# The low parts of the GLA gates' weights, made on GpSimd instead of VectorE

## The chip, the core and the metric

The kernel runs on one core of a Trainium2 chip. The metric is the device time of one execution in microseconds (us). The profile names the engines PE (TensorE; PEld is its weight load), DVE (VectorE), ACT (ScalarE), POOL (GpSimd) and SP (SyncE, which here does little but issue DMAs). Each engine works through a queue of its own in the order in which the program holds it: an instruction that waits holds up all that stand behind it.

## The reference

The program is a two-layer network on 512 tokens of width 1024, all in float32. Layer 0 mixes the tokens with an RWKV-7 recurrence (8 heads) and with gated linear attention (GLA, 4 heads), layer 1 with differential attention; a SwiGLU block follows each. The part that matters here:

```python
proj = h @ w_in
p_rkv = proj[..., :3 * RW_WIDTH]
gq, gk, gv, gg = jnp.split(proj[..., 3 * RW_WIDTH:], ...)
...
o = gla_chunked(...)                                  # 4 heads, 128 wide each
o_b = o.reshape(Bsz, T, GLA_VW).astype(h.dtype) * jax.nn.silu(gg)
return jnp.concatenate([o_a, o_b], axis=-1) @ w_out
```

`gg` is the GLA gates: 512 columns, four tiles of 128. `o_a` is the output of the RWKV-7 recurrence.

## The kernel before, in words

**Matrix products.** A float32 product is made of three faster ones. Each operand is split into a high part (a copy in a shorter format) and a low part (the rest): `split` makes the high part with a cast on ScalarE (L96, tile `whi`) and the low part with a subtraction on VectorE (L97, tile `wlo`). `mm3` then issues three matmuls: high by high (L107), high weight by low activation (L108), low weight by high activation (L109). `form_a` walks over the 1024 rows of a weight tile; in the first mixer it takes them in two pieces of 512 columns (256 KB), so that each tile of 128 outputs costs two DMAs (L84), two casts, two subtractions and 24 matmuls. The loaded pieces (`wraw`) live in a ring of three buffers: the fourth load can't start before the first piece's cast and subtraction are done. `whi` and `wlo` have rings of four here.

**The first mixer.** Token shifts and projections of RWKV-7 run chunk by chunk over four groups of two heads (class `Chunk`: `decays`, `project`, `key`, `receptance`, `value`, `gram`). In `shifted` the projection comes out of PSUM on VectorE (L501) and is scaled on ScalarE (L504, tile `d`); `value` uses `d` on VectorE (L556, L559); `gram` makes small matmuls (L547 belongs to `receptance`, L571 to `gram`), masks them on VectorE (L577) and moves them on ScalarE (L579 to L608).

**The two solves.** The recurrence needs the inverses of unit lower triangular blocks. `solve` computes them by 31 steps of a product (L633) and a sum (L635). The first solve (chunks 0 and 1, tiles `xl0`, `al0`, `tmp0`) runs on GpSimd, the second (chunks 2 and 3, tiles `xl2`, `al2`, `tmp2`) on VectorE. The second begins with a transpose (L624), which needs the last L608 of `gram` of chunk 3, and ends with a transpose (L638) and copies into place (L644, six of them on ScalarE).

**The gates.** `gla_gates` makes the four tiles of `gg`: a `form_a` each, a product with the row norms (L454), Silu (L455), a product with the GLA output on GpSimd (L458), and a DMA back to memory (L459). Its code stands between the last `gram` and the second solve. The output stage `rwkv_out` (L661, L663, L668, L670, ...) takes over the PSUM banks and the SBUF space of the gates, so it starts when they are done. Its copies into `st.fv` are L677 and L678, its state chain is L709, L712 (tile `H`, ScalarE), L714 (tile `S`, VectorE), and then L718 and L719 in turn.

**Order.** The code is recorded in program order; a scheduler with a cost model of its own then sets the order of each engine's queue, and adds the semaphore waits. So moving one kind of instruction to another engine can change the order of others.

Of the kernel before, what the change touches and what calls it, by code (L numbers as in the profile page):

```python
# [9 lines left out]
F32 = mybir.dt.float32  # L10
# [50 lines left out]
def dbank(g):  # L61
    return bank(g, "pd")
# [25 lines left out]
def split(g, raw, into=None):  # L88

    nc, n = g.nc, raw.shape[-1]  # L90
    if into:
        hi, lo = into
    else:
        hi = g.wp.tile([P, g.wn], F32R, name="whi", bufs=3 if g.wn > 512 else 4)[:, :n]
        lo = g.wp.tile([P, g.wn], F32R, name="wlo", bufs=3 if g.wn > 512 else 4)[:, :n]
    nc.scalar.copy(hi, raw)  # L96
    nc.vector.tensor_sub(lo, raw, hi.bitcast(F32))  # L97
    return hi, lo


# [347 lines left out]
def gla_gates(g, pool, ob):  # L448
    nc = g.nc
    for h in range(4):  # L450
        pg = dbank(g)
        form_a(g, pg, g.ap["win"][16 + h], g.xhi, g.xlo)
        gg = pool.tile([P, T], F32, name="gg", bufs=2)
        nc.vector.tensor_mul(gg, pg, g.rstd)  # L454
        nc.scalar.activation(gg, gg, AF.Silu)  # L455
        o = pool.tile([P, T], F32, name="o", bufs=2)
        nc.sync.dma_start(o, ob[h])
        nc.gpsimd.tensor_mul(o, o, gg)  # L458
        nc.sync.dma_start(ob[h], o)  # L459
# [722 lines left out]
def build(tc, ap, cols, dbg=None, parts=("mix0", "ffn0", "attn", "ffn1", "final")):  # L1182
    with ExitStack() as ctx:
        g = setup(ctx, tc, ap, dbg)
        g.cols, g.ahead = cols, 0
        if "mix0" in parts:
            mixer0(g)
        else:
            for c in range(KD):
                g.nc.sync.dma_start(g.xT[:, c], ap["xT"][:, c])  # L1190
        acts_pool(g, ctx, "xs")
        g.tbp = ctx.enter_context(tc.tile_pool(name="tb", bufs=1))
        g.tb = g.tbp.tile([P, NH_A, T], F32, name="tb")
        g.sqs = ctx.enter_context(tc.tile_pool(name="sqs", bufs=1))
        psum_pool(g, ctx, "ps", pd=3, sc=2, pt=2, po=1)
        weights_pool(g, ctx, 1024)
        if "ffn0" in parts:
            ffn(g, 0, bias_tables)
        if "attn" in parts:
            g.ahead = 120  # L1200
            attention(g)
            g.ahead = 0
        if "ffn1" in parts:
            ffn(g, 1, last=down_norm)
# [107 lines left out]
```

## Time and profile before

| | |
|---|---|
| time, median of 3 runs | 1336.83 us (1335.76 to 1337.07) |
| the profiled execution | 1336.43 us, its span 1334.6 us |
| PE busy | 1302.7 us, 98% |
| DVE busy | 701.3 us, 53% |
| ACT busy | 563.9 us, 42% |
| POOL busy | 216.3 us, 16% |
| L97 (all of them) on DVE | 252.4 us, 240 instructions |
| granted clock of PE, mean over the span | 0.992 |

Busy times overlap, since the engines run side by side. A share of the whole span says little about one stage: the stage of this change lies between 200 and 300 us, and is read there. Times of rows are counted from the start of the span. 1.83 us of the profiled execution lie around the span.

### The profile page before, as it was taken

To read this page: it belongs to the slowest core of one execution; us is meant where nothing else is said; L and a number is where in the kernel's file an instruction comes from. 1 tells how busy PE (TensorE), PEld (TensorE's weight loads), DVE (VectorE), ACT (ScalarE), POOL (GpSimd) and SP (SyncE) were. 2 spreads that over 40 slices of the span, in tenths; PEclk is the share of its full clock that TensorE was granted. 3 is DMA by queue.
4 is the path that set the end of the run, shared out by engine and by line. 5 is a ranking of instruction groups with operands and counts; after the bars stand their busy time and mean duration, and the time that the engine had idled before them with its cause. 6 is when DMAs were issued, how large, how long until landed. Compare 5 with 4: busy or idle time off the path is not lost.

```text
span 1334.6 us, 17753 instructions
## 1 busy us (share of the span) xinstructions
PE 1302.7 (98%) x6856; PEld 1065.9 (80%) x6856; DVE 701.3 (53%) x1197; ACT 563.9 (42%) x957; POOL 216.3 (16%) x205
## 2 busy tenths in 40 slices
PE   8999989899999999999999999999999999999998
PEld 6788767687878888888888887887888888888886
DVE  7465778954554433334434258888643434433342
ACT  5555866353443222223334347777432322322232
POOL 3011084211511110011112001110201110011110
PEclk9999989899999999999999999999999999999999
DMA  6222222423645323433234332211333323553331
GB/s 196 66 64 87 72 72 87 156 72 108 233 140 163 95 77 97 115 104 99 75 88 125 96 95 64 52 46 46 110 102 102 93 75 97 148 127 98 101 100 63
DMA packets 52719, 133.72 MB, mean 100 GB/s; under 512 B 6067, under 2 KB 8499, under 8 KB 52636
## 3 DMA queue, kind: packets, MB, share of 16 engines
q1 hardware_dynamic: 51772, 131.43, 32.8%
q8 instruction: 54, 0.88, 0.3%
q10 hardware_dynamic: 864, 1.17, 0.2%
q14 instruction: 29, 0.24, 0.1%
HBM read 121.74 MB, written 11.36 MB: 100 GB/s over the span
## 4 chain that ended last, share of the span: by engine, by line
PE 90%; DVE 7%; ACT 2%; issue 1%; DMA 0%; DVEq 0%; ACTq 0%
PE pd L109 24%; PE pd L108 24%; PE pd L107 24%; PE po L1054 2%; DVE wlo L97 1%; DVE tmp L633 1%; DVE xl L635 1%; PE sc L1029 1%; PE sc L1030 1%; PE o L109 1%; PE o L108 1%; PE o L107 1%; PE pt L1050 0%; PE o L675 0%; PE po L108 0%
## 5 line engine op out<-in xcount | busy, mean ns | idle before, releaser
L96 ACT CAST whi<-wraw 128x1024 fp32r<-128x1024 f32 (+2 forms) x240 | 210.4, 879 | 521.1 <-PE pd L108 302.0
L109 PE MATMUL pd<-xhi,wlo 128*128 128x512 f32 x1032 | 406.6, 394 | 0.0
L107 PE MATMUL pd<-xhi,whi 128*128 128x512 f32 x1032 | 405.6, 393 | 0.9 <-ACT xhi L188 0.9
L108 PE MATMUL pd<-xlo,whi 128*128 128x512 f32 x1032 | 405.8, 393 | 0.0
L97 DVE TENSOR_TENSOR wlo<-wraw,whi 128x1024 fp32r<-128x1024 f32 (+2 forms) x240 | 252.4, 1054 | 137.1 <-ACT whi L96 136.2
L107 PEld LDWEIGHTS pd<-xhi,whi 128*128 128x128 f32 x1032 | 193.8, 188 | 42.1 <-ACT xhi L188 1.3
L108 PEld LDWEIGHTS pd<-xlo,whi 128*128 128x128 f32 x1032 | 193.8, 188 | 41.1 <-issue 0.2
L109 PEld LDWEIGHTS pd<-xhi,wlo 128*128 128x128 f32 x1032 | 193.9, 188 | 40.4
L231 POOL TENSOR_TENSOR hlo<-h,hhi 128x512 fp32r<-128x512 f32 x44 | 67.3, 1529 | 546.3 <-ACT hhi L230 546.3
L227 DVE TENSOR_TENSOR ut<-pd,rstd 128x512 f32<-128x512 f32 x44 | 30.4, 692 | 146.3 <-PE pd L109 146.3
L107 PE MATMUL pd<-hhi,whi 128*128 128x512 f32 x264 | 102.7, 389 | 0.0
L108 PE MATMUL pd<-hlo,whi 128*128 128x512 f32 x264 | 102.7, 389 | 0.0
L109 PE MATMUL pd<-hhi,wlo 128*128 128x512 f32 x264 | 102.7, 389 | 0.0
L224 DVE TENSOR_TENSOR gt<-pd,rstd 128x512 f32<-128x512 f32 x44 | 30.4, 692 | 123.5 <-PE pd L109 121.4
L108 PEld LDWEIGHTS pd<-hlo,whi 128*128 128x128 f32 x264 | 49.6, 188 | 10.3
L107 PEld LDWEIGHTS pd<-hhi,whi 128*128 128x128 f32 x264 | 49.5, 188 | 10.3
L109 PEld LDWEIGHTS pd<-hhi,wlo 128*128 128x128 f32 x264 | 49.5, 188 | 10.3
L1034 ACT ACTIVATE s<-s,mn 128x384 f32<-128x384 f32 (+3 forms) x64 | 35.7, 559 | 21.4 <-DVE mn L1031 20.8
L230 ACT CAST hhi<-h 128x512 fp32r<-128x512 f32 x44 | 27.4, 622 | 35.5 <-DVE h L229 35.5
L240 DVE TENSOR_TENSOR xT<-pd,xT 128x512 f32<-128x512 f32 x24 | 16.6, 692 | 46.2 <-PE pd L109 46.2
L1010 POOL TENSOR_TENSOR qst<-q,qst 64x512 fp32r<-64x512 f32 x8 | 13.2, 1646 | 167.9 <-DVE qst L1008 167.9
L157 POOL TENSOR_TENSOR ssum<-nsq,ssum 128x512 f32<-128x512 f32 x21 | 31.5, 1498 | 49.9 <-ACT nsq L153 49.4
(384 smaller groups left out, 1837.4 us busy)
## 6 DMA issues: line engine op xcount, KB each, us to landing
wraw<-in_gate SPq DMA_DIRECT2D x44, 512.0 KB, 3.7
wraw<-in_up SPq DMA_DIRECT2D x44, 512.0 KB, 3.6
wraw<-in_win SPq DMA_DIRECT2D x40, 256.0 KB, 2.7
wraw<-in_down SPq DMA_DIRECT2D x24, 384.0 KB, 3.1
wraw<-in_wqk SPq DMA_DIRECT2D x16, 512.0 KB, 3.6
wraw<-in_down SPq DMA_DIRECT2D x24, 320.0 KB, 2.8
wraw<-in_downt SPq DMA_DIRECT2D x10, 512.0 KB, 3.7
xT<-in_xT SPq DMA_DIRECT2D x16, 256.0 KB, 3.9
```

The costliest lines, as they stand in the source:

```text
L96: nc.scalar.copy(hi, raw)
L97: nc.vector.tensor_sub(lo, raw, hi.bitcast(F32))
L107: nc.tensor.matmul(out, lhsT=lhi, rhs=rhi, start=start, stop=False)
L108: nc.tensor.matmul(out, lhsT=lhi, rhs=rlo, start=False, stop=False)
L109: nc.tensor.matmul(out, lhsT=llo, rhs=rhi, start=False, stop=stop)
L157: (nc.vector if c in fast else nc.gpsimd).tensor_add(ss, sq, first if c == 1 else ss)
L224: nc.vector.tensor_mul(gt, pg, rstd)
L227: nc.vector.tensor_mul(ut, pu, rstd)
L230: nc.scalar.copy(hhi[:, n], h)
L231: nc.gpsimd.tensor_sub(hlo[:, n], h, hhi[:, n].bitcast(F32))
L1034: nc.scalar.activation(s[:, m, :L], s[:, m, :L], AF.Exp, bias=mn[:, m:m + 1], scale=-1.0, accum_out=sm[:, m:m + 1])
L1054: nc.tensor.matmul(po[:, qb * P:qb * P + P], lhsT=att[:, b * P:b * P + P], rhs=v[:, b, h * P:h * P + P], start=b == 0, stop=b == qb)
```

## The change

```diff
@@ split
     nc.scalar.copy(hi, raw)
-    nc.vector.tensor_sub(lo, raw, hi.bitcast(F32))
+    g.low.tensor_sub(lo, raw, hi.bitcast(F32))
     return hi, lo
@@ gla_gates
     for h in range(4):
         pg = dbank(g)
+        g.low = nc.gpsimd
         form_a(g, pg, g.ap["win"][16 + h], g.xhi, g.xlo)
+        g.low = nc.vector
         gg = pool.tile([P, T], F32, name="gg", bufs=2)
@@ build
-        g.cols, g.ahead = cols, 0
+        g.cols, g.ahead, g.low = cols, 0, g.nc.vector
```

Eight subtractions of 128x512 (two for each of four tiles) change from VectorE to GpSimd. All others stay. Lines behind L451 of the kernel before stand two or three lines lower in the changed one (L458 is L460 there, L627 is L629, L633 is L635, L635 is L637, L644 is L646, L678 is L680, L712 is L714).

**First place: GpSimd's queue, from the end of the first solve to the last product of a gate.** `tmp0` and `xl0` belong to the first solve, `ga` is cleared for the inverses, `o` is a gate's GLA output. Before:

```order
L633 TENSOR_TENSOR tmp0_1560<-al0_1554,xl0_1551 128x31
L635 TENSOR_TENSOR xl0_1551<-xl0_1551,tmp0_1560 128x31
L627 MEMSET ga_1002 128x512 x4
L458 TENSOR_TENSOR o_2174<-o_2174,gg_2171 128x512
L458 TENSOR_TENSOR o_2218<-o_2218,gg_2215 128x512
L458 TENSOR_TENSOR o_2262<-o_2262,gg_2259 128x512
```

With the change:

```order
L637 TENSOR_TENSOR xl0_1551<-xl0_1551,tmp0_1560 128x31
L629 MEMSET ga_1002 128x512 x2
L97 TENSOR_TENSOR wlo_2138<-wraw_2135,whi_2137 128x512
L97 TENSOR_TENSOR wlo_2156<-wraw_2153,whi_2155 128x512
L97 TENSOR_TENSOR wlo_2182<-wraw_2179,whi_2181 128x512
L97 TENSOR_TENSOR wlo_2200<-wraw_2197,whi_2199 128x512
L629 MEMSET ga_1002 128x512
L97 TENSOR_TENSOR wlo_2226<-wraw_2223,whi_2225 128x512
L629 MEMSET ga_1002 128x512
L97 TENSOR_TENSOR wlo_2244<-wraw_2241,whi_2243 128x512
L460 TENSOR_TENSOR o_2174<-o_2174,gg_2171 128x512
L97 TENSOR_TENSOR wlo_2270<-wraw_2267,whi_2269 128x512
```

The eighth L97 (`wlo_2288`) follows the last row shown. All eight stand behind the whole first solve and two of the four memsets.

**Second place: ScalarE's queue at `value` of chunk 3.** `whi_2199` is the high part of the fourth gate piece, whose load (`wraw_2197`) takes the buffer of the first piece; `d_2044` is what `value` waits for. Before:

```order
L96 CAST whi_2181<-wraw_2179 128x512
L528 ACTIVATE a_1798<-a_1798,oka_282,vec_64 128x512
L96 CAST whi_2199<-wraw_2197 128x512
L504 ACTIVATE d_2044<-p_2041,omr_280 128x512
L96 CAST whi_2225<-wraw_2223 128x512
L579 COPY n21_1004<-ga_1002 32x2x128
L608 COPY dg_1013<-ga_1002 32x2x128 x2
```

With the change:

```order
L96 CAST whi_2181<-wraw_2179 128x512
L530 ACTIVATE a_1798<-a_1798,oka_282,vec_64 128x512
L96 CAST whi_2199<-wraw_2197 128x512
L506 ACTIVATE d_2044<-p_2041,omr_280 128x512
L581 COPY n21_1004<-ga_1002 32x2x128
L610 COPY dg_1013<-ga_1002 32x2x128 x2
```

The cast of `whi_2199` stands ahead of `d_2044` in both; the cast of `whi_2225` went behind the L608s.

**Third place: ScalarE's queue at the end of the second solve.** `dg` holds the solve's result; `o0` is a PSUM bank of the output stage of chunk 0, `xT` its result, `H_2542` its part of the state chain. Before:

```order
L676 COPY r_1000<-o0_2471 128x4x64
L678 COPY xT_63<-o0_2471 64x256
L712 COPY H_2542<-o0_2525 128x512
L908 CAST ghi_2410<-o_3189 128x512
L644 COPY ga_1002<-dg_1013 32x2x4x32 x6
```

With the change:

```order
L678 COPY r_1000<-o0_2471 128x4x64
L646 COPY ga_1002<-dg_1013 32x2x4x32 x6
L680 COPY xT_63<-o0_2471 64x256
L910 CAST ghi_2410<-o_3189 128x512
L714 COPY H_2542<-o0_2525 128x512
```

The six copies that wait for the second solve stood behind chunk 0's last copies, and now stand ahead of two of them. In VectorE's queue the gates' last L454 stood behind 34 instructions of the second solve's steps, and now stands behind 41.

## Rows read from the trace of the kernel before

**Rows 1.** Busy time by stretch: start:end, length, engines' busy us, PEclk, DMA share, GB/s.

```profile
212.00:216.00 4.00, 3.91 (x17) 2.82 (x15) 4.00 (x8) 1.95 (x3) 3.61 (x8) 1.00 0.40 131
...
244.00:248.00 4.00, 0.52 (x3) 0.08 (x1) 3.90 (x7) 1.35 (x3) 1.31 (x1) 1.00 0.44 140
...
268.00:272.00 4.00, 2.89 (x16) 2.78 (x17) 3.04 (x7) 3.54 (x8) 0.81 (x1) 0.76 0.00 0
272.00:276.00 4.00, 4.00 (x74) 3.80 (x75) 2.08 (x6) 2.15 (x6) 0.00 (x0) 0.81 0.46 135
```

**Rows 2.** The chain in order of time, 196 to 300 us: start, us, what.

```profile
229.34 0.63 ACT whi L96
229.99 0.69 DVE wlo L97
...
233.84 1.39 DVE wlo L97
...
237.25 0.60 DVE wlo L97
```

**Rows 3.** Timeline of POOL: start, us, engine, line, operation, tiles [idle before, releaser].

```profile
214.92 0.25 POOL L635 TENSOR_TENSOR xl<-xl,tmp 128x31 f32<-128x31 f32 x1
215.11 0.99 POOL L627 MEMSET ga<- 128x512 f32 x2
...
238.00 1.30 POOL L458 TENSOR_TENSOR o<-o,gg 128x512 f32<-128x512 f32 x1 [3.31 <-ACT gg L455]
```

**Rows 4.** The page's costliest groups: a subtraction of the same shape and types on POOL.

```profile
L231 POOL TENSOR_TENSOR hlo<-h,hhi 128x512 fp32r<-128x512 f32 x44 | 67.3, 1529 | 546.3 <-ACT hhi L230 546.3
```

**Rows 5.** The page's DMA issues: KB each, median us to landing.

```profile
wraw<-in_win SPq DMA_DIRECT2D x40, 256.0 KB, 2.7
```

**Rows 6.** Timeline of DVE, SP's DMA queue, ACT and PE around the gates' first piece.

```profile
204.08 1.02 DVE L97 TENSOR_TENSOR wlo<-wraw,whi 128x512 fp32r<-128x512 f32 x1 [1.17 <-ACT whi L96]
...
205.13 3.72 SPq L84 DMA_DIRECT2D wraw<-in_win  x2
...
213.34 0.61 ACT L96 CAST whi<-wraw 128x512 fp32r<-128x512 f32 x1
...
213.41 0.40 PE L109 MATMUL pd<-xhi,wlo 128*128 128x512 f32 x1
...
215.38 0.72 ACT L504 ACTIVATE d<-p,omr 128x512 f32<-128x512 f32 x1 [1.44 <-DVE p L501]
...
216.60 0.87 DVE L556 SCALAR_TENSOR_TENSOR vs<-p,vec,d 128x256 f32<-128x256 f32 x2
...
217.39 0.68 DVE L97 TENSOR_TENSOR wlo<-wraw,whi 128x512 fp32r<-128x512 f32 x1
...
224.49 2.00 DVE L624 STREAM_TRANSPOSE al<-dg 128x1024 f32<-128x1024 f32 x1 [1.37 <-ACT dg L608]
```

**Rows 7.** Timeline of DVE in the second solve.

```profile
237.77 0.37 DVE L633 TENSOR_TENSOR tmp<-al,xl 128x207 f32<-128x207 f32 x1
238.17 1.36 DVE L635 TENSOR_TENSOR xl<-xl,tmp 128x207 f32<-128x207 f32 x1
...
244.50 1.49 DVE L633 TENSOR_TENSOR tmp<-al,xl 128x252 f32<-128x252 f32 x1
246.03 0.42 DVE L635 TENSOR_TENSOR xl<-xl,tmp 128x252 f32<-128x252 f32 x1
```

**Rows 8.** Timelines of DVE and ACT where the solve ends and the state chain begins.

```profile
262.23 0.37 ACT L678 COPY xT<-o 64x256 f32<-64x256 f32 x1 [0.48 <-DVE xT L677]
263.84 0.59 ACT L712 COPY H<-o 128x512 f32<-128x512 f32 x1 [1.25 <-PE o L709]
...
264.60 1.25 DVE L638 STREAM_TRANSPOSE dg<-xl 128x1024 f32<-128x1024 f32 x1
...
265.88 3.83 ACT L644 COPY ga<-dg 32x256 f32<-32x256 f32 x6 [0.80 <-DVE dg L638]
...
268.00 0.86 DVE L714 COPY S<-H 128x64 f32<-128x64 f32 x1
```

## The prediction

> **What bounds the kernel now.** Over the whole span PE is the bound, busy for 98% of it. That says nothing about the stage of this change, so read first the busy times by stretch. From 212 to 216 us VectorE is busy for 4.00 of 4.00 us, and from 244 to 248 for 3.90, while PE works 0.52 of them [rows 1]. Here VectorE sets the pace and PE waits. The chain in order of time agrees: the gates' subtractions (L97) stand on it one by one, and so does a cast they wait for [rows 2]. So taking eight of them off VectorE looks like a gain. Whether it is one depends on three things that the shares don't show: when GpSimd is free, what waits for the first of its results, and what VectorE does while GpSimd reads.
>
> The sum is made against the profiled execution, 1336.43 us (span 1334.6 us and 1.83 us around it), which is 0.4 us under the median of the runs.
>
> **First term: the second solve starts later, +4.0 us.** In the new queue all eight subtractions stand behind the first solve and two memsets. That solve ended at 214.92 + 0.25 us and the memsets at 215.11 + 0.99 = 216.10 us [rows 3]. VectorE made the first gate piece's low part at 204.08 us [rows 6]; GpSimd can't begin before about 216.1. How long it takes: L458, a two-input instruction of the same size, took 1.30 us [rows 3]; L231, a subtraction with the same shapes and types, 1.53 us in the mean of 44 [rows 4]. While VectorE is idle I take 1.30, so the low part is there at 217.4.
>
> Who waits for it? PE, whose first matmul with it came at 213.41 us [rows 6], but more so the load of the fourth piece: the buffers are a ring of three, and in the trace that load left at 205.13 us, just when the first subtraction (204.08 + 1.02) was over [rows 6]. Now it leaves at 217.4, lands 2.7 us later [rows 5], at 220.1, and ScalarE casts it in 0.61 us [rows 6], until 220.7. Behind that cast, in ScalarE's queue, stands L504 of `value`, 0.72 us long, which ran at 215.38 [rows 6]. It ends at 221.4, so VectorE's L556, which began at 216.60 [rows 6], begins 4.8 us later. Against this, two subtractions go from between L556 and the masks (one of the two is in [rows 6]); a subtraction that doesn't wait costs the chain 0.6 us [rows 2], so -1.2. And GpSimd's fourth subtraction runs from 220.7 to 222.0 and meets L556 at 221.4, which holds it for up to 0.6 us (next term); I take 0.4. Sum +4.0: `gram` and with it L624, at 224.49 us [rows 6], come 4.0 us later. The ends: +3.0, if the first solve finishes 0.7 us earlier because three VectorE subtractions no longer run beside it and L556 isn't held, and +4.6 with 1.53 us for the subtraction and the full 0.6.
>
> **Second term: inside the second solve, +0.2 us.** Three of the gates' subtractions stood there: 0.69, 1.39 and 0.60 us of the chain [rows 2]. Of the 1.39 half was waiting behind an L458 on GpSimd, which another instruction will now do in its place, so 0.69, 0.69 and 0.60: -2.0. VectorE also waited for two casts; one is on the chain with 0.63 us [rows 2], and I take -0.4 for each. Together -2.8.
>
> What comes in their place is the row that decides. L635 at 238.17 us took 1.36 us, where the instruction before it, of the same size, took 0.37; from 238.00 us GpSimd had been at L458 for 1.30 us [rows 3, 7]. At 244.50 it is 1.49 against 0.42 [rows 7]. So a step of the solve that starts while GpSimd works on two inputs ends only after GpSimd does: 0.99 and 1.07 us lost. In the new order the last three subtractions on GpSimd fall into the solve: 3 x 1.0 = +3.0. The fifth runs beside the two transposes, for which no row shows a hold: 0, with 1.0 as its upper end. Sum +0.2, ends -2.8 (nothing is held) and +1.9 (that 1.0, and each 0.23 us longer, as L231 is).
>
> The Trainium skill, SBUF — State Buffer, section "SBUF: two separate sides", says that the ports VectorE shares with GpSimd are locked exclusively for a whole instruction and that the loser fully blocks. The trace agrees in kind but not to the end: L635 ended 0.23 us after L458 and not its own 0.37 after it; by the rule each hold would cost 0.14 us more and the sum would grow by 0.4.
>
> So the solve's last transpose, L638, goes from 264.60 [rows 8] to 268.8 us.
>
> **Third term: a changed order on ScalarE, +3.9 us.** Before, chunk 0's L678 and L712 stood ahead of the six L644 that wait for the solve; now these are ahead. L638 takes 1.25 us, until 270.05, the six copies 3.83 us, until 273.9, then L678 0.37 us, until 274.3 [rows 8]. From the end of L678 to L712 there lay 1.24 us of PE work (262.60 to 263.84), and L712 takes 0.59 [rows 8]: 276.1 us. Then L714 starts, which started at 268.00 [rows 8]. Its shift is 8.1 us, 3.9 more than the solve's. The gates' own way is no later: seven more steps at 0.42 us stand ahead of the last L454, and with the first two terms that is 7.1 us.
>
> **Fourth term: what comes back, -1.7 us.** In 268 to 276 us the granted clock was 0.76 and 0.81 [rows 1], so PE ran at 1.2 GHz for (0.24 + 0.19) x 4 / 0.5 = 3.4 of these 8 us, on chunk 0's and 1's matmuls. The same work comes later now and, at 2.4 GHz, takes 1.7 us less. Ends: 0 (the lower clock comes too) and -3.4 (further work that stood ahead of it is done by then). A new spell of waiting, from 213.4 to 217.6 us, can lower the clock in `gram`; that stage then waits for ScalarE and VectorE, so I take 0 for it, with 1.7 as its upper end.
>
> Once the later stages start, PE is the bound, and what it is late by stays. Sum: 4.0 + 0.2 + 3.9 - 1.7 = **+6.4 us**, 1342.8 us by the profiled execution, 1343.2 on the scale of the median; I write 1343.
>
> **Rivals.**
>
> *Faster: GpSimd is in time.* If the first low part were ready when PE reaches it, VectorE would only lose work: -1.2 before the solve and -2.8 in it, -4.0 us, 1332.8. It decides at 213.41 us, when PE reaches it [rows 6]. For it: VectorE is full in 212 to 216 us [rows 1], three subtractions fewer beside the first solve speed that up, and GpSimd is idle after it. Against: with 0.99 us of memsets and 1.30 of subtraction behind it, the solve would have to end by 211.1, 4 us before 215.17 [rows 3], and the holds of [rows 7] would have to be free of cost. 6%. The Trainium skill, Perfetto Trace Analysis, section "Optimizing Scalar/DVE Operations", holds that with VectorE saturated it may make sense to move work even to GpSimd, which is this case; it adds that the shared port may spoil that, as the trace's rows do here.
>
> *Slower by less: no hold.* If subtractions don't hold VectorE as L458 does, the first term is 3.6 and the second -2.8; L638 comes 0.8 later, and with the third and fourth the end is 0.8 + 3.9 - 1.7 = +3.0, 1339.8. Against it are both rows of [rows 7]. 12%.
>
> *No change: the end hangs on something else.* If chunk 0's chain isn't what sets the end, only the solve's 4.2 us count, less up to 3.4: +0.8 to +2.5, 1337.6 to 1339.3. 7%.
>
> *Slower by more: the clock.* If the new spell takes 1.7 us in `gram` and nothing comes back in 268 to 276 us, +9.8, 1346.6. 9%.
>
> **How the numbers follow.** The forecast itself, 1341 to 1345, gets 66%. A measurement of this kernel can tell about 0.2% from no change, 2.7 us: the bounds are 1334.2 and 1339.5. The forecast and the clock lie above, half of the no-hold case too: 81% slower. Its other half and the no-change case: 13%. Faster: 6%. The range must take in the forecast, the no-hold case and most of the clock's: 1338.5 to 1346.5; out of it are the faster case, part of the no-change case, and what lies above.
>
> **What would show it.** The first L97 on GpSimd at about 216 us, PE idle from 213.4 until then, and the load of the fourth piece just behind it. L504 at 220.7 and L624 at 228 to 229 us. In the solve, steps of 1.3 to 1.5 us wherever a GpSimd L97 or L458 runs. L638 at about 269 us, and L714 (the one for `S`) at about 276. In the stages behind the mixer everything as before, 6 us later. Wrong would be: a first GpSimd L97 before 213, solve steps under 0.5 us beside GpSimd's subtractions, or L714 later by 8 us with the end later by less than 3.

## The result and the profile after

With the change the kernel takes 1344.10 us in the median of 4 runs (1343.24 to 1344.33), beside 1336.45 us before (4 runs, 1335.76 to 1337.07): ratio 1.0056, 95% interval 1.0043 to 1.0068. It is 7.65 us slower, where +6.4 was forecast. The profiled execution took 1344.33 us, its span 1342.5 us, 7.9 us more than that of before. The lines of the kernel before from L454 on all stand two further down now: L454, L624, L638 and L714, for instance, are L456, L626, L640 and L716. The medians of this document leave out one execution, of the run e11 below, that lasted 2615.38 us.

The page's costliest groups. The eight subtractions have left VectorE, and PE's wait for one of them is the only idle time that the page puts ahead of L109:

```profile
L109 PE MATMUL pd<-xhi,wlo 128*128 128x512 f32 x1032 | 407.2, 395 | 3.3 <-POOL wlo L97 3.3
...
L97 DVE TENSOR_TENSOR wlo<-wraw,whi 128x1024 fp32r<-128x1024 f32 (+2 forms) x232 | 251.0, 1084 | 128.5 <-ACT whi L96 127.9
```

**Where the start is lost.** Timeline of GpSimd (POOL), which answers to [rows 3]:

```profile
215.08 0.31 POOL L637 TENSOR_TENSOR xl<-xl,tmp 128x31 f32<-128x31 f32 x1
215.34 0.98 POOL L629 MEMSET ga<- 128x512 f32 x2
216.29 3.72 POOL L97 TENSOR_TENSOR wlo<-wraw,whi 128x512 fp32r<-128x512 f32 x3
220.80 1.27 POOL L97 TENSOR_TENSOR wlo<-wraw,whi 128x512 fp32r<-128x512 f32 x1 [0.80 <-ACT whi L96]
...
236.85 1.42 POOL L97 TENSOR_TENSOR wlo<-wraw,whi 128x512 fp32r<-128x512 f32 x1 [5.59 <-ACT whi L96]
238.79 1.30 POOL L460 TENSOR_TENSOR o<-o,gg 128x512 f32<-128x512 f32 x1 [0.53 <-ACT gg L457]
240.05 2.81 POOL L97 TENSOR_TENSOR wlo<-wraw,whi 128x512 fp32r<-128x512 f32 x2
```

Three low parts stood ready to be made and waited for the first solve and two memsets. What waits behind them, in the timelines of SP's DMA queue, ScalarE and PE (they answer to [rows 6]):

```profile
217.57 1.56 SPq L84 DMA_DIRECT2D wraw<-in_win  x2
...
220.11 0.62 ACT L96 CAST whi<-wraw 128x512 fp32r<-128x512 f32 x1 [6.39 <-DMA wraw<-in_win]
220.63 0.72 ACT L506 ACTIVATE d<-p,omr 128x512 f32<-128x512 f32 x1
...
217.60 0.80 PE L109 MATMUL pd<-xhi,wlo 128*128 128x512 f32 x1 [3.26 <-POOL wlo L97]
```

**The solve and the order behind it.** Timeline of VectorE, which answers to [rows 6 to 8]:

```profile
207.88 0.69 DVE L503 TENSOR_TENSOR p<-pd,rstd 128x512 f32<-128x512 f32 x1 [0.88 <-PE pd L109]
...
221.39 1.36 DVE L558 SCALAR_TENSOR_TENSOR vs<-p,vec,d 128x256 f32<-128x256 f32 x2 [4.84 <-ACT d L506]
...
228.57 2.02 DVE L626 STREAM_TRANSPOSE al<-dg 128x1024 f32<-128x1024 f32 x1 [1.37 <-ACT dg L610]
...
238.91 1.42 DVE L635 TENSOR_TENSOR tmp<-al,xl 128x207 f32<-128x207 f32 x1
240.36 1.35 DVE L637 TENSOR_TENSOR xl<-xl,tmp 128x207 f32<-128x207 f32 x1
241.75 1.36 DVE L635 TENSOR_TENSOR tmp<-al,xl 128x220 f32<-128x220 f32 x1
...
268.61 1.25 DVE L640 STREAM_TRANSPOSE dg<-xl 128x1024 f32<-128x1024 f32 x1
...
276.00 0.20 DVE L716 COPY S<-H 128x64 f32<-128x64 f32 x1 [2.25 <-ACT H L714]
```

And of ScalarE, which answers to [rows 8]: the six copies now stand between the last transpose and chunk 0's L680 and L714.

```profile
269.89 3.86 ACT L646 COPY ga<-dg 32x256 f32<-32x256 f32 x6 [0.24 <-DVE dg L640]
273.77 0.37 ACT L680 COPY xT<-o 64x256 f32<-64x256 f32 x1
...
275.39 0.59 ACT L714 COPY H<-o 128x512 f32<-128x512 f32 x1 [0.61 <-PE o L711]
```

**PE's account.** Windows of after (columns: length, then busy us of PE, PE's weight loads, VectorE, ScalarE and GpSimd, PEclk, DMA share, GB/s), and the same two stretches of before:

```profile
244.00:268.00 24.00, 14.24 (x82) 12.54 (x81) 22.95 (x48) 6.90 (x13) 6.76 (x6) 0.86 0.47 152
268.00:290.00 22.00, 19.57 (x331) 18.16 (x330) 13.52 (x36) 13.45 (x28) 1.04 (x1) 0.92 0.26 77
```

```profile
244.00:268.00 24.00, 16.34 (x182) 14.84 (x180) 22.90 (x52) 9.97 (x21) 5.91 (x6) 0.86 0.44 142
268.00:290.00 22.00, 20.82 (x252) 18.25 (x253) 12.21 (x31) 11.18 (x21) 1.86 (x2) 0.92 0.12 37
```

PE idles 2.1 us more in the first stretch and 1.3 in the second, and the mean granted clock (the column PEclk) of each is what it was. But a low clock costs only where PE is at work. This way of counting carries the experiments, so here is how it is done. PE is the bound of the kernel, so a later end must be either idle time of PE or busy time at half its clock. Both can be summed over windows of 1 us from 204 to 290 us: idle is length less busy, and the loss to the clock is busy time times (1 - PEclk). Before has 10.3 + 4.8 = 15.1 us of the two, after 16.8 + 4.9 = 21.8 (before rounding 15.06 and 21.76): +6.7. By stretch the idle time grows by 3.0 us in 212 to 224, 2.1 in 244 to 268 and 1.3 in 268 to 290; the loss to the clock grows by 1.5, shrinks by 1.3 (3.0 to 1.7) and stays at 1.7. What is missing to 7.9 was mostly there before the change's place: the L503 above starts at 207.88, the same step of before (L501) at 207.12:

```profile
207.12 0.69 DVE L501 TENSOR_TENSOR p<-pd,rstd 128x512 f32<-128x512 f32 x1 [0.67 <-PE pd L109]
```

In the fourteen profiles of this case that step starts between 206.8 and 208.2 us, in kernels with and without the change. The offset is older than the change's place: an earlier run of the same line starts at 153.96 us before and at 154.75 with the change. So some 0.8 us of this profile's difference is such an offset.

### The profile page after: what moved, and what is told of

It reads as the page before. It is cut to its first block, busy times and chain, and to the rows that moved or that the text cites. A ratio compares the mean times of both kernels' runs of the same rounds, so it can differ in the third digit from the quotient of the medians.

```text
span 1342.5 us, 17755 instructions
## 1 busy us (share of the span) xinstructions
PE 1304.2 (97%) x6856; PEld 1066.6 (79%) x6856; DVE 703.3 (52%) x1189; ACT 564.5 (42%) x957; POOL 226.3 (17%) x213
## 4 chain that ended last, share of the span: by engine, by line
PE 87%; DVE 5%; POOL 3%; ACT 2%; issue 2%; DMA 1%; SPq 0%; ACTq 0%; POOLq 0%; DVEq 0%
PE pd L107 24%; PE pd L109 24%; PE pd L108 24%; POOL xl L637 2%; POOL tmp L635 2%; PE po L1056 1%; DVE tmp L635 1%; PE sc L1031 1%; PE sc L1032 1%; PE o L109 1%; PE o L108 1%; PE o L107 1%; PE o L720 0%; DVE xl L637 0%; PE pt L1052 0%
## 5 line engine op out<-in xcount | busy, mean ns | idle before, releaser
L109 PE MATMUL pd<-xhi,wlo 128*128 128x512 f32 x1032 | 407.2, 395 | 3.3 <-POOL wlo L97 3.3
L97 DVE TENSOR_TENSOR wlo<-wraw,whi 128x1024 fp32r<-128x1024 f32 (+2 forms) x232 | 251.0, 1084 | 128.5 <-ACT whi L96 127.9
L109 PEld LDWEIGHTS pd<-xhi,wlo 128*128 128x128 f32 x1032 | 194.1, 188 | 44.1 <-POOL wlo L97 3.7
L109 PE MATMUL pd<-hhi,wlo 128*128 128x512 f32 x264 | 102.7, 389 | 0.0
L107 PEld LDWEIGHTS pd<-hhi,whi 128*128 128x128 f32 x264 | 49.6, 188 | 10.3
L109 PEld LDWEIGHTS pd<-hhi,wlo 128*128 128x128 f32 x264 | 49.5, 188 | 10.2
```

The lines of the kernel that those rows point to most:

```text
L97: g.low.tensor_sub(lo, raw, hi.bitcast(F32))
L107: nc.tensor.matmul(out, lhsT=lhi, rhs=rhi, start=start, stop=False)
L109: nc.tensor.matmul(out, lhsT=llo, rhs=rhi, start=False, stop=stop)
```

## Experiments

My theory had four terms: a late start through GpSimd's queue, holds of VectorE that eat what the solve gains, ScalarE's changed order, and something that comes back. The rivals: holds cost nothing; only the holds cost; only the order; only the clock. The experiments undo one of these at a time. Where an order had to be moved, instructions were tied behind a chosen one of the same engine (`issue_after`). Nothing else was changed in the code, but the scheduler could still order other instructions anew, and in e4 and e10 it did.

| run | median us | against before, 95% | profiled us | L626 | S | PE idle + clock loss, 204 to 290 us |
|---|---|---|---|---|---|---|
| before | 1336.45 | | 1336.43 | 224.49 | 268.00 | 10.3 + 4.8 |
| the change | 1344.10 | 1.0043 to 1.0068 | 1344.33 | 228.57 | 276.00 | 16.8 + 4.9 |
| e1, late gates alone | 1339.42 | 1.0011 to 1.0031 | 1341.46 | 225.77 | 271.79 | 14.1 + 5.1 |
| e2, ScalarE's order | 1341.76 | 1.0026 to 1.0051 | 1341.62 | 228.50 | 272.98 | 13.5 + 5.7 |
| e3, GpSimd's order | 1340.54 | 1.0022 to 1.0047 | 1343.21 | 226.28 | 274.48 | 15.2 + 5.7 |
| e4, multiplications on VectorE | 1330.78 | 0.9946 to 0.9969 | 1330.29 | 224.29 | 263.51 | 9.2 + 0.0 |
| e5, one cast | 1339.78 | 1.0017 to 1.0039 | 1341.56 | 227.30 | 274.77 | 15.4 + 3.6 |
| e6, seven spare matmuls | 1348.45 | 1.0075 to 1.0101 | 1348.78 | 229.12 | 280.75 | 16.1 + 5.0 |
| e7, solve's tail late | 1336.24 | 0.9983 to 1.0000 | 1336.44 | 224.16 | 264.64 | 9.2 + 6.2 |
| e8, early gates, no hold | 1341.76 | 1.0026 to 1.0052 | 1340.50 | 226.06 | 267.27 | 11.5 + 7.9 |
| e9, four spare matmuls | 1344.76 | 1.0045 to 1.0069 | 1344.76 | 228.89 | 276.28 | 15.6 + 3.0 |
| e10, spare matmuls in before | 1341.09 | 1.0019 to 1.0042 | 1341.19 | 224.12 | 271.46 | 9.5 + 5.7 |
| e11, late gates on top of e4 | 1336.78 | 0.9990 to 1.0011 | 1335.67 | 225.84 | 267.58 | 9.1 + 3.6 |
| e12, last gate ahead, on top of e4 | 1332.54 | 0.9956 to 0.9979 | 1332.53 | 225.53 | 263.95 | 8.4 + 1.7 |

L626 and S stand for the second solve's first transpose and for chunk 0's copy to S, whatever their line in that kernel, in the profiled execution, whose time stands beside them and can lie off the median by up to 2.7 us. Each interval is against executions of the kernel before taken beside that experiment (medians 1336.62 for e1 to e4, 1336.50 for e5 to e8, 1336.67 for e9 to e12). The last column less 15.1, with the offset at 207 us (and, in e6, e9 and e10, the spare matmuls' own 6.3, 3.7 and 5.3 us), gives the profiled execution's difference to before within 0.7 us in every run.

### The late start: e3, e5, e1

e3 puts the last eight steps of the first solve behind the first four low parts, on GpSimd alone:

```diff
@@ split (of the changed kernel)
-    g.low.tensor_sub(lo, raw, hi.bitcast(F32))
+    ins = g.low.tensor_sub(lo, raw, hi.bitcast(F32))
+    if g.low is nc.gpsimd and g.rest:
+        with g.tc.issue_after(ins.ins):
+            next(g.rest.pop(0))
@@ solve
     for s in range(31):
+        if not cs[0] and s in (23, 24, 26, 28):
+            yield
@@ mixer0
+        g.rest = [first] * 4
         with tc.tile_pool(name="gates", bufs=1, side="right") as sp:
```

> The whole change, with another order on GpSimd: the last eight steps of the first solve stand behind the first four low parts, so that these are made at 204.6, 207.6, 211 and 214 us instead of 217 to 222. Theory: the late start goes. Two subtractions less on VectorE (-1.2) against holds in key and value of up to 1.0 each: L626 at 223.5 to 225.5. Solve as with the change, last transpose at 264 to 265.5, ScalarE's order as with the change, S at 271.5 to 273. End 1339.5 to 1341. Rival, the start is late because GpSimd is slower at a subtraction, not because of its queue: L626 stays at 227 or later, end 1343 or more.

L626 is at 226.28, of which 0.7 is offset (the step of 207.12 is at 207.80): 2.3 us earlier than with the change, and 1.1 later than before. The median is 3.6 us under the change's, 1340.54, inside what was expected. The profiled execution, 1343.21, is the slowest of five and only 1.1 under: it has 1.7 us less idle time and loses 0.8 more to the clock, and its S, at 273.8 without the offset, comes later than the expected 271.5 to 273. So GpSimd's queue made most of the late start, not its slowness. The 1.1 that stay are a balance: VectorE's steps from 206.5 to 218.7 us take 12.4 us in sum, where the same steps of before take 9.5 (+2.9, holds); value's first step waits 0.8 us for d; and the four subtractions that no longer stand among and behind them give 2.6 back. The timelines of GpSimd and VectorE in this run show one place, and the last line the same step before:

```profile
213.04 1.75 POOL L97 TENSOR_TENSOR wlo<-wraw,whi 128x512 fp32r<-128x512 f32 x1
```

```profile
212.66 0.98 DVE L532 TENSOR_TENSOR kk<-kk,a 128x512 f32<-128x512 f32 x1
213.67 1.67 DVE L540 TENSOR_TENSOR bkt<-kk,en 128x512 f32<-128x512 f32 x1
```

```profile
213.26 0.78 DVE L535 TENSOR_TENSOR bkt<-kk,en 128x512 f32<-128x512 f32 x1
```

L540 (L535 of before) took 0.78 us before; here it runs until 215.3, 0.5 us behind the end of GpSimd's subtraction (214.8).

e5 leaves GpSimd alone and moves one cast on ScalarE, that of the fourth gate piece, behind value's d:

```diff
@@ split (of the changed kernel)
-    nc.scalar.copy(hi, raw)
+    g.pieces += g.low is nc.gpsimd
+    if g.pieces == 4:
+        with g.tc.issue_after(g.scaled.ins):
+            nc.scalar.copy(hi, raw)
+    else:
+        nc.scalar.copy(hi, raw)
@@ Chunk.shifted
-        nc.scalar.mul(d, p[:, 1:], self.m0.omr[:, n:n + 1])
+        g.scaled = nc.scalar.mul(d, p[:, 1:], self.m0.omr[:, n:n + 1])
...
```

> The whole change, with one cast moved on ScalarE: that of the fourth gate piece stands behind the product d of value (L506, here L511) instead of ahead of it. GpSimd's queue stays as it is, so the first low part is still made at 216 to 217.5 us and PE still waits for it. Theory (the late start comes through the load of the fourth piece and the cast that ScalarE waits for, not through PE's wait): d at 214 to 216 instead of 220.6, value's steps at 216 to 217, and L626 (here L631) at 225.4 to 226, held back only by the copies that still stand behind the cast; 2.6 to 3.1 earlier than with the change. The end 2.5 to 3 earlier, 1341 to 1341.6. Rival, the start hangs on PE's wait for the low part: L626 stays at 228 to 228.6, end at 1344.

The first half came as expected: d at 216.53 and value's step at 217.28, which is before's 216.60 with the offset. The second half did not. Timeline of VectorE in this run:

```profile
217.28 1.92 DVE L563 SCALAR_TENSOR_TENSOR vs<-p,vec,d 128x256 f32<-128x256 f32 x2 [0.79 <-ACT d L511]
220.97 0.76 DVE L566 TENSOR_TENSOR d<-pb,vs 128x256 f32<-128x256 f32 x2 [1.77 <-PE pb L554]
...
227.30 2.02 DVE L631 STREAM_TRANSPOSE al<-dg 128x1024 f32<-128x1024 f32 x1 [1.37 <-ACT dg L615]
```

The next step waits for a product (L554) that stands on PE behind the gates' matmul, and that one waits for the low part until 217.55. L631 is only 1.3 us earlier than with the change. So the low part was waited for on two ways of almost the same length: the fourth load and its cast, which I had priced, and PE's own queue, which I had named and not priced. Only the first was taken away here, and the second alone keeps 2.1 of the 3.3 us. The median is 4.3 us under the change's, more than the start explains; the profiled execution, at 1341.56, is 2.8 under, and this kernel's executions lie between 1338.9 and 1343.9. In the profile S is 1.2 us earlier, and the account shows the rest: no lower clock in 268 to 290 us (3.6 lost in all instead of 4.9), on top of 1.4 less idle. Why it stays away there is open; the section on the clock comes back to it.

e1 gives the first two gates back to VectorE:

```diff
@@ gla_gates (of the changed kernel)
-        g.low = nc.gpsimd
+        g.low = nc.gpsimd if h >= 2 else nc.vector
```

> Only the last two gates' four low parts are made on GpSimd; the first two gates' four stay on VectorE. My theory (late start through GpSimd's queue, holds that eat the relief, changed order on ScalarE): the low parts that GpSimd makes are not behind the first solve, so L626 is back at 224.5 to 225.3 us. In the solve, three subtractions less (-2.0) and two waits for casts less (-0.8) against three holds of 1.0: L640 at 264.6 to 265.6. On ScalarE the six L646 stand only ahead of chunk 0's copy to H: S at about 270.3 where it was 268.0. End 1338.0 to 1339.0. Rival, subtractions do not hold VectorE: L640 at 262, end 1335.5 to 1336. Rival, all the cost lies in the holds, not in the late start: end 1340 or more, with L626 at 224.5.

With 0.9 of offset taken off, L626 is at 224.9 and S at 270.9. The late start is gone. The solve, from L626 to L640, takes 40.26 us, where it took 40.11 before and 40.04 with the change: in all three the holds cost what the subtractions had cost. That speaks against the rival "no hold", by which it would have been 37.3. The end is at 1339.42, 0.4 us above the expected stretch; the executions of this kernel lie between 1337.8 and 1342.4.

### What a hold costs: e4, e11

The solve's steps in both kernels (lines of the view by line, 224 to 269 us; columns: busy us, mean ns, idle before). Before:

```profile
L635 DVE TENSOR_TENSOR xl<-xl,tmp 128x31 f32<-128x31 f32 (+15 forms) x31 | 12.6, 407 | 0.8
L633 DVE TENSOR_TENSOR tmp<-al,xl 128x31 f32<-128x31 f32 (+15 forms) x31 | 12.3, 398 | 0.8
L97 DVE TENSOR_TENSOR wlo<-wraw,whi 128x512 fp32r<-128x512 f32 x7 | 5.5, 785 | 0.9 <-ACT whi L96 0.9
```

After:

```profile
L635 DVE TENSOR_TENSOR tmp<-al,xl 128x31 f32<-128x31 f32 (+15 forms) x31 | 16.4, 531 | 0.8
L637 DVE TENSOR_TENSOR xl<-xl,tmp 128x31 f32<-128x31 f32 (+15 forms) x31 | 12.6, 408 | 0.9
L97 DVE TENSOR_TENSOR wlo<-wraw,whi 128x512 fp32r<-128x512 f32 x4 | 2.7, 683 | 0.0
```

The same 62 steps take 4.1 us more (24.9 to 29.0), and three subtractions with their waits take 3.7 less (2.8 and 0.9). Four more steps are held: three by L97, and one by L460 at 238.79, whose counterpart before (the first L458) held a subtraction (1.39 us instead of 0.69, at 233.84) and no step.

e4 takes GpSimd's multiplications, and their holds with them, out of the second solve of the kernel before:

```diff
@@ gla_gates (of the kernel before)
-        nc.gpsimd.tensor_mul(o, o, gg)
+        nc.vector.tensor_mul(o, o, gg)
```

> The kernel before, with the gates' four multiplications (L458) on VectorE instead of GpSimd. VectorE has four instructions of 0.6 to 0.7 us more in the second solve, and GpSimd none beside it. Theory (a two-input instruction on GpSimd holds a step of the solve for 1.0 us): no step of the solve takes over 0.5 us, the solve is 1.2 to 1.6 us shorter, and the end is at 1334.9 or somewhat earlier, as chunk 0's S now stands ahead of the solve's last steps. Rival, the long steps have another cause, or the holds cost the chain nothing: the solve is 2.5 us longer and the end 1337.5 to 1339.

1330.78 us, 5.8 under before and 13.3 under the change: the best kernel of this study. No step of the solve takes over 0.7 us in its timeline (0.5 was expected), and the view by line (224 to 272 us) has the price of a hold:

```profile
L635 DVE TENSOR_TENSOR xl<-xl,tmp 128x31 f32<-128x31 f32 (+15 forms) x31 | 10.9, 352 | 0.7
L633 DVE TENSOR_TENSOR tmp<-al,xl 128x31 f32<-128x31 f32 (+15 forms) x31 | 10.7, 346 | 0.6
...
L458 DVE TENSOR_TENSOR o<-o,gg 128x512 f32<-128x512 f32 x4 | 2.7, 684 | 0.7 <-ACT gg L455 0.7
```

The 62 steps take 21.6 us, 3.3 less than before and 7.4 less than with the change. Before has four held steps (three by L458, one by GpSimd's product dw) and the change eight: 0.8 and 0.9 us each in the mean, where a multiplication on VectorE costs 0.7. Nor is e4 quite free of holds: two steps beside the products dw take 0.69 and 0.64 us, where the steps next to them take 0.37 and 0.25, and counted without these a hold costs 1.0. The direction was right; the solve's last transpose, though, is not earlier but 1.5 us later (266.14), since more of chunk 0's instructions stand ahead of it now. The gain is far larger than expected (1334.9 or somewhat less), and the reason is on PE. Timeline of PE and windows of this run:

```profile
247.47 3.81 PE L661 MATMUL o<-r,ga 128*128 128x128 f32 x32 [3.13 <-DVE gg L454]
```

```profile
248.00:256.00 8.00, 6.57 (x57) 6.28 (x56) 7.43 (x17) 2.85 (x7) 2.85 (x3) 1.00 0.53 163
```

and the same of before:

```profile
250.34 6.73 PE L661 MATMUL o<-r,ga 128*128 128x128 f32 x32 [5.81 <-DVE gg L454]
```

```profile
248.00:256.00 8.00, 5.66 (x26) 5.67 (x27) 7.62 (x16) 1.70 (x3) 2.54 (x3) 0.60 0.31 100
```

All of the rwkv part waits for the last gate's step on VectorE (L454). It came at 249.60 before and comes at 246.65 here, for two reasons. Two steps held by L458 (238.17 and 244.50) and one held subtraction (1.39 us instead of 0.69, at 233.84) stood ahead of it, some 2.8 us in all, for which three multiplications stand there now (0.6 each from start to start, 1.8). And the scheduler put 30 of the solve's steps ahead of it instead of 34: four at 0.46, another 1.8. The two make 2.8; the trace has 2.95. PE's wait shrinks from 5.8 to 3.1 us, and after the shorter wait the granted clock stays at 1.00, where it was at 0.50 from 249.6 to 256.4 before. S follows at 263.51, 4.5 us earlier.

e11 is e4 with the last two gates' subtractions on GpSimd (e1's edit with e4's), so that held steps come back.

> The multiplications on VectorE (the run of 1330.8 us), and of the change the last two gates' four subtractions on GpSimd: beside the solve, GpSimd now does these four and nothing else on two inputs. The barest exchange: four times 0.6 to 0.7 us of VectorE's own work against four holds of 1.0 us. Theory: the last gate's step at 247.5 to 248 instead of 246.65, three or four long steps in the solve, end 1 to 1.5 us later, 1331.8 to 1332.3; if PE's longer wait for that step brings the lower clock back, up to 1335. Rival, subtractions on GpSimd are free for VectorE: last gate's step at 244.5 to 245, end 1328.5 to 1330.

1336.78 us in the median of ten executions (1335.42 to 1340.02), 6.0 above e4. The solve's 62 steps take 24.4 us, 2.8 more than in e4, for three holds; three subtractions had cost VectorE 2.1 there. The timeline shows three held steps (231.63, 235.28 and 237.52 us, 1.26, 1.44 and 1.33 us), the last gate's step at 250.29, 2.5 later than in e4 after 1.15 of offset, PE's wait at 5.1 us, and then the lower clock, as the expectation had it for its bad case and 1.8 us beyond it. Part of the later gate step is again order: 34 solve steps stand ahead of it, as before, and not e4's 30 (four at 0.46, 1.8 us). The holds and that order are not told apart here; the solve's own total, 2.8 against 2.1, is the hold's alone. Windows:

```profile
248.00:252.00 4.00, 0.97 (x4) 0.97 (x5) 3.90 (x10) 0.63 (x1) 0.00 (x0) 0.50 0.58 184
252.00:256.00 4.00, 4.00 (x26) 4.00 (x25) 3.73 (x10) 0.27 (x1) 0.23 (x1) 0.65 0.43 131
```

e8 asks whether the idea is good away from the solve: e3's edit for the first two gates alone, with e4's multiplications.

> The change where it should hurt least: low parts of the first two gates on GpSimd, with its queue ordered so that they stand ahead of the first solve's last eight steps; the last two gates' low parts and the four multiplications on VectorE, so that GpSimd does nothing on two inputs beside the second solve. Theory: GpSimd's four subtractions hold VectorE's steps in key and value for as much as they relieve it, L626 0.5 to 1.5 us later than before; no long steps in the solve; end 1331 to 1333, no better than with the multiplications on VectorE alone (1330.8). Rival, the idea is good away from the solve: end 1328 to 1330.

It is not: 1341.76. L626 is at 226.06 (1.4 above e4's after 0.3 of offset, as expected), for the same reason as in e3: VectorE's steps in key and value are held as long as they were relieved. The expected end was missed by 9 us, though. Of the 10.2 us that PE loses more than in e4, 2.3 are idle and 7.9 are the clock (1.7 in 212 to 224, 6.2 in 268 to 290, where it is at 0.50 from 270 to 283). The delay and the long spell of the lower clock came together here; that the one made the other is not shown. I had put no clock into this expectation.

### The order on ScalarE and VectorE: e2, e7, e12

e2 puts the six copies back behind chunk 0's copy to H:

```diff
@@ solve (of the changed kernel)
     xt = xt.rearrange("p (t a c i) -> p t a c i", a=2, c=RC, i=4)
+    if cs[0]:
+        yield
@@ rwkv_out
-    nc.scalar.copy(H, ph)
+    g.last = nc.scalar.copy(H, ph)
@@ mixer0
...
+            def tail():
+                with tc.issue_after(g.last.ins):
+                    next(second, None)
...
@@ interleave
...
         n += 1
+        if n == lag - 1:
+            tail()
```

> The whole change, with ScalarE's order put back: the six L646 of the second solve (L648 here) stand behind chunk 0's copy to H. Theory: the late start and the holds are untouched, L626 at 228 to 229 and the last transpose at 268 to 269 us, but S follows it after 3.4 us, as before the change: at 272.0 instead of 276.0, and the end is 3.9 us earlier than with the change, 1340.2. If the spell of lower clock does not come at all, another 1.7 us: 1338.5. Rival, the end hangs on the solve or on chunk 2, not on chunk 0's S: end within 1 us of 1344.1, though S is earlier.

H is copied at 271.72 instead of 275.39, and S is at 272.98: 3.0 us earlier, not 3.9, since VectorE's own additions to G now stand ahead of it until 273.1. The end is 2.3 us earlier, where 3.9 was expected. So the order is a cost of its own; the third term is shown, at three quarters of its size in S. The account has PE idle 3.4 us less and the clock 0.8 worse (2.8 lost in 212 to 224, instead of 1.5, ahead of this edit's place).

e7 changes the order in the kernel before, on VectorE alone: the solve's last seven steps, its transpose and its copies behind chunk 0's S.

```diff
@@ solve (of the kernel before)
     for s in range(31):
+        if cs[0] and s == 24:
+            yield
@@ rwkv_out
-    nc.vector.tensor_copy(S[:, 1], H[:, 0])
+    g.last = nc.vector.tensor_copy(S[:, 1], H[:, 0])
@@ mixer0
...
+            def tail():
+                with tc.issue_after(g.last.ins):
+                    for _ in second:
+                        pass
...
```

> The kernel before, with VectorE's order changed alone: the second solve's last seven steps, its last transpose and its copies stand behind chunk 0's S. The multiplications stay on GpSimd, so four steps are held as before. This parts the two things that the run with the multiplications on VectorE did at once (no holds, and S ahead of the solve's end). If the order made its gain: S at 264.5 to 265.5 instead of 268.0 and the end 3 us earlier, 1333.5. If the holds made it: S no earlier than 267 and the end at 1336 to 1337. My theory gives the order about half: 1333 to 1335.

S is 3.4 us earlier, at 264.64, and the median is where it was: 1336.24, where 1333 to 1335 was expected. Its executions lie between 1333.9 and 1337.1 us, five of eleven below 1334.5; the profiled one, 1336.44, is not among these. In the account it has the same 9.2 us of idle time as e4, and 6.2 us of clock loss where e4 has none; the two profiled executions differ by 6.15 us. Windows of e7:

```profile
248.00:256.00 8.00, 6.05 (x30) 6.05 (x31) 7.62 (x16) 1.71 (x3) 2.93 (x3) 0.57 0.35 115
282.00:288.00 6.00, 6.00 (x18) 3.42 (x18) 1.56 (x4) 2.27 (x4) 0.00 (x0) 0.57 0.00 0
```

Here L454 still stands behind the held steps (249.22), PE still waits 5.75 us for it, and the clock falls. So an earlier S alone does not give e4's gain; the best execution of e7 is still 3.1 us above e4's median. What e4 has over the profiled e7 is the clock: 2.8 of the 6.2 us are lost behind that wait, which is 3.1 us in e4 and is followed by no fall there. The other 3.4 are lost in a second spell, from 282.9 to 289.7 us, behind a wait of PE of only 1.0 us, and no run here shows what brings it. The first wait is shorter in e4 through the holds that are gone and the four steps that moved; which of the two would have sufficed was not tried.

e12 goes one step further from e4: the solve's steps from the fourteenth on behind the last gate's step.

> The multiplications on VectorE, and the solve's steps from the fourteenth on stand behind the last gate's step (L454) instead of partly ahead of it. Theory: that step, for which PE waits with everything that follows, starts as soon as the last gate's products are done, at 244.6 to 245.2 instead of 246.65; PE's wait there shrinks from 3.1 to about 1.3 us; S at 261.7 to 262.2 instead of 263.5; end 1329.0 to 1329.5 where it was 1330.8. Rival, the end hangs on chunk 2 and the solve's end by now: no change, 1330.3 to 1331.3.

PE's wait there is 1.45 us, as expected, and S is 0.8 us earlier (1.24 of offset taken off). The median is 1332.54, with executions from 1329.9 to 1335.1, e4's from 1330.3 to 1332.6: no gain. In the profile, PE waits 2.24 us for S at 264.28, and the clock is at 0.50 behind it, until about 268.6. e4 stays the best version.

### The clock: e6, e9, e10

e6 and e9 fill the wait after which the change's clock falls (271.8 to 274.2 us) with spare matmuls:

```diff
@@ rwkv_out (of the changed kernel; 7 in e6, 4 in e9)
+    if c == 0:
+        spare = dbank(g)
+        with g.tc.issue_after(mm.ins):
+            for _ in range(7):
+                mm = nc.tensor.matmul(spare, lhsT=g.ident, rhs=st.gr[:, 0, 0, 0:2].rearrange("p c i f -> p (c i f)"),
+                                      start=True, stop=True)
...
+            with g.tc.issue_after(mm.ins):
+                nc.tensor.matmul(ph[hr, q], lhsT=st.bk[:, c, q, hr], rhs=st.fv[:, e, m // 2, c, 2 * (m % 2) + hp],
+                                 start=True, stop=True)
```

> The whole change, with seven spare matmuls on PE (their result is read by nobody) right after chunk 0's products for G and ahead of its products for H, where PE idled from 271.8 to 274.2 us. Theory: the lower clock after 275 us follows that idle time; with PE at work it does not come, the granted clock in 272 to 280 is 1.00 instead of 0.91 and 0.66, and the 1.7 us that it costs there come back: 1342.4. Rival, the lower clock there costs nothing because PE waits anyhow: same rows at 1.00, end at 1344 within 0.7. Rival, it does not follow the idle time: clock as with the change, end 1344 to 1345.

Seven took 6.3 us, 0.9 each, and pushed H to 280.13: badly sized, end 1348.45. The clock stays at 1.00 from 268 to 290 us.

> The run with spare matmuls again, with four of them instead of seven: one took 0.90 us there, so that seven lasted 3 us beyond the wait that they were to fill, and chunk 0's copy to H came 4.7 us later. Four fill 3.6 us, from 270.9 to 274.5, when the products for H can start. Theory: the granted clock stays at 1.00 in 272 to 280, H is where the change has it (275.4 to 276), and PE's 1.7 us come back: end 1342.4, up to 1343. Rival, PE waits for S anyhow and the clock there costs nothing: same rows, end 1344 to 1345.

With four, H is at 275.64 and the clock as the theory has it. Windows of the change, then of e9:

```profile
272.00:276.00 4.00, 1.81 (x35) 1.75 (x36) 1.71 (x4) 3.32 (x7) 1.04 (x1) 0.91 0.00 0
276.00:280.00 4.00, 4.00 (x26) 3.90 (x24) 2.33 (x6) 2.06 (x6) 0.00 (x0) 0.66 0.01 2
```

```profile
272.00:276.00 4.00, 3.89 (x42) 2.25 (x41) 2.31 (x6) 3.83 (x8) 1.04 (x1) 1.00 0.00 0
276.00:280.00 4.00, 3.10 (x28) 2.85 (x26) 2.29 (x7) 1.71 (x4) 0.00 (x0) 1.00 0.44 133
```

So with the wait filled the fall at 275 us does not come. That such a wait alone makes it fall is not shown, and e5 speaks against it: there PE waits just as long at the same place, and the clock stays. Timeline of PE and windows of e5:

```profile
272.95 1.15 PE L716 MATMUL o<-xT,bkt 128*64 128x64 f32 x32 [2.43 <-ACT xT L685]
```

```profile
272.00:276.00 4.00, 3.05 (x48) 2.94 (x49) 1.71 (x5) 3.30 (x7) 0.66 (x1) 1.00 0.00 0
```

In e9 the end did not come earlier, 1344.76: the spare matmuls took 3.7 us and displaced ten products of chunk 1 (L670) that PE had done in that stretch. In 268 to 290 us the change has 2.4 us of idle time and 1.7 of clock loss, e9 1.0, 0, and 3.7 of spare work: 4.1 against 4.7. The 1.7 are thus counted from rows, not shown in the end.

e10 tries the same in the kernel before, with six behind the last gate.

> The kernel before, with six spare matmuls on PE behind the last gate's products, which fill the wait for the last gate's step on VectorE (244.5 to 250.3 us). In the kernel before, the granted clock falls to 0.50 at 249.8 and stays there until 256.4. Theory: with PE at work the clock stays at 1.00, and chunk 0's first products take 3 us less; but S stands on VectorE behind the solve's last transpose, which doesn't move, so S stays at 268.0 +- 0.3 and the end within 1 us of 1336.5. Rival, the half clock there sets the end: 1333.5.

It does not answer its question. With PE at work, the clock did not fall at 249.6, as it does before. But the order that the scheduler then chose was another: chunk 0's next products waited 2.9 us (252.1 to 255.0) for ScalarE's copies, the clock was at 0.50 from 255.6 to 265.8, and on ScalarE the six L644 stood ahead of H, which was copied at 270.84 (263.84 before). S at 271.46 is 3.5 us later and the end 4.4: by accident a second showing of the third term. What the first half-clock spell alone costs the kernel before stays open.

## Why the prediction was right, and where it was wrong

**What bounds the stage, and the decision: right.** The three questions that it asked (when GpSimd is free, what waits for its first result, what VectorE does while GpSimd reads) are the three costs that the runs found. Slower, by 7.65 us where 6.4 was written. One reading in it was wrong: in 212 to 216 us PE was busy for 3.91 of 4.00 us [rows 1] and did not wait; of the two stretches named, VectorE sets the pace in 244 to 248 alone.

**First term, +4.0: measured 4.08, of which 0.76 is offset, so 3.3.** GpSimd free at 216.29 (216.10 forecast), load at 217.57 (217.4), cast done at 220.73 (220.7), L558 at 221.39 (221.4), L626 at 228.57 (228.5). These agree with the offset in them; without it the first solve ends 0.5 us earlier against the rest of the program, which was the reason given for the lower end. (The ends add up to +2.9 and +4.4 from the terms that it gives, not +3.0 and +4.6.) The way through the load and the cast was the longer one, but e5 shows that PE's queue alone would have kept all but 1.3 us of it. "Who waits for it?" deserved two prices.

**Second term, +0.2: measured -0.1** (40.04 us from L626 to L640, 40.11 before). The price of a hold, 1.0 us, was right; there were four more held steps, not three, against 3.7 us of relief, not 2.8, and chunk 0's two additions to G no longer stand ahead of L640. That the two misses cancel is luck.

**Third term, +3.9: measured +4.0** (S 7.39 us behind L640, 3.40 before). It was read from the order and the rows ahead of it, and e2 shows it by taking it away.

**Fourth term, -1.7: the step that failed.** "The same work comes later now and, at 2.4 GHz, takes 1.7 us less." It did come later, and the lower clock came with it: 0.50 from 275.3 to 278.7 us, 1.7 us lost, as in 270.1 to 273.5 before. The mean granted clock in 268 to 290 us is 0.92 in both kernels. I had treated the spell as tied to a time, when its row shows it behind PE's idle time (266.3 to 269.1 us before, 271.8 to 274.2 after), and the third term, which I had just priced, makes such idle time. In e9, with that wait filled, the spell does not come; in e5 the same wait is followed by none, so a wait alone does not settle it, and what else does stays open. The term's upper bound, 0, was the right value for 268 to 276 us, and it is right for the whole stretch by a balance that was not forecast: 1.5 us more are lost to the clock in 212 to 224, and 1.3 less in 244 to 268, where more of the low clock now falls into PE's idle time; the rest of the difference between 6.4 and 7.9 is the offset, less 0.7 in the first term and 0.3 in the second.

**The rivals.** "GpSimd is in time" fell with the first L97 at 216.29. "No hold" fell with e1 and e11. "The end hangs on something else" does not hold for this change: S moved by 8.0 us and the end by 7.9, and e2, which brings S back by 3.0, brings the end back by 2.3. The two are not tied in general, as e7 and e8 show. "The clock" was half right: nothing came back in 268 to 276 us, but the new spell in 217 to 221 us cost the chain nothing extra: e2 loses 2.8 us to the clock there, the change 1.5, and their L626 agree within 0.1 us once the offsets are taken off.

## What to carry to other kernels

Price a move from VectorE to GpSimd by what GpSimd does to VectorE meanwhile: here 0.8 to 1.0 us per held step against 0.6 to 0.7 us of VectorE's own work, so that where VectorE sets the pace, the opposite move (e4) was the gain. An in-order queue makes an instruction as late as the last one ahead of it, so look up what stands there on the new engine, and price every queue in which something waits behind the result. And where PE is the bound, keep an account of its idle time and of its time at half clock, run by run: a wait that gets shorter can gain twice, and one that gets longer can lose twice.

## What the runs showed of the hardware that I had not expected

- The hold works both ways. GpSimd's subtraction of 128x512 took 1.27 and 1.29 us in the change where VectorE was idle or at a transpose as it began (220.80 and 229.51), and 1.72 to 1.75 in e3 where it began beside a VectorE step with two inputs. Of the pair shown from e3, L532 ran until 213.64, GpSimd's subtraction ended 1.15 us after it, at 214.79, and VectorE's L540 0.55 us after that. In the solve, held steps ended 0.24 us behind GpSimd (238.79 + 1.30 = 240.09 and 238.91 + 1.42 = 240.33). The Trainium skill, SBUF — State Buffer, section "SBUF: two separate sides", says that whichever engine starts first keeps the shared ports for its whole instruction and the other fully blocks. The rows of the solve agree in kind, and so does e3's place if the step ahead is counted in: L532 blocks the subtraction, and the subtraction blocks L540.
- Whether PE's clock falls is not told by the length of the wait alone: it stayed at 1.00 after 3.1 us (e4, 244.4 to 247.5), 3.6 us (e8, 247.5 to 251.1) and 2.4 us (e5, 270.5 to 273.0), and fell after 5.8 us (before), but also after 2.4 us (the change, 271.8 to 274.2), 2.2 us (e12) and 1.0 us (e7, 279.8 to 280.8).
- Executions of one and the same kernel differ by whole microseconds with their mean granted clock: twelve of e1 run from 1337.8 us (0.996) to 1342.4 us (0.990), eleven of e7 from 1333.9 (0.994) to 1337.1 (0.991), and eighteen of the kernel before, taken beside e9 to e12, from 1335.7 (0.994) to 1340.2 (0.991). A difference of 2 us between two single executions of these kernels says little by itself.
